# Idle tiles of queries, keys, values and probabilities take raw weight blocks in layer 0, and the loads at the change of layers are spaced two steps apart

## The chip, the core and the metric

The kernel runs on one core of a Trainium2 chip. Its engines are TensorE (PE, matmuls; PEld is its weight load), VectorE (DVE), ScalarE (ACT), GpSimd (POOL, unused here but for four constants) and the SyncE queue (SP), which issues most DMAs. The metric is the device time of one execution in microseconds (us), by the median of several runs. All times below come from a profiled execution of the kernel before or from the times of its runs.

## The reference

A trunk of two layers over 256 positions of width 2048, in float32. Layer 0 mixes by trailing-window means, layer 1 by causal attention within one block of 256 positions (there is only one block, so every selected block is masked away). Both layers have a memory branch, a SiLU gate for each branch, one output projection, a residual and a layer norm:

```python
def reference(x, mem, w_in, w_out, w_mem_kv, ln_g, ln_b, pool_w, pool_scale, w_kv_shared):
    h = x
    split_at = [BRANCH_WIDTH, 2 * BRANCH_WIDTH, 2 * BRANCH_WIDTH + MEM_WIDTH]   # 1536, 3072, 3584
    for i in range(DEPTH):                                                      # 2
        if i == N_A_LAYERS:                                                     # 1
            k_blocks, v_blocks, k_mean = moba_shared_kv(h, w_kv_shared)
        u = h @ w_in[i]                                                         # 2048 x 4096
        branch_in, gate_b, mem_q, gate_m = jnp.split(u, split_at, axis=-1)
        if i < N_A_LAYERS:
            branch = multiscale_pool(branch_in, pool_w[i], pool_scale[i])
        else:
            branch = moba_attention(branch_in, k_blocks, v_blocks, k_mean)
        mem_o = memory_attention(mem_q, mem, w_mem_kv[i])
        mixed = jnp.concatenate([branch * jax.nn.silu(gate_b), mem_o * jax.nn.silu(gate_m)], axis=-1)
        y = mixed @ w_out[i]                                                    # 2048 x 2048
        h = layer_norm(DEEPNORM_ALPHA * h + y, ln_g[i], ln_b[i])
    return h
```

Nearly all of the work is the projections: 256 rows times some 36 million weights, each weight read once from HBM.

## The kernel before

**Precision by halves.** Each float32 operand is split into a high and a low part of the type float32r (`split`, L100): ACT copies the source into the high part (L102), DVE subtracts that from the source for the low part (L103). A product is then three matmuls: high x high, high x low, low x high.

**Items and steps.** The weights are cut into blocks of 128 x 1024 float32 (512 KB). Each block is an *item* of the list `items`; the program handles them in order, one *step* for an item (`run`, L200). Step i does this, in program order: prepare item i + 3 (`prep_piece`: ACT and DVE split it into `wh`, `wl`, of which there are four pairs); issue on SP the raw loads that the plan has for step i; let TensorE consume item i (twelve matmuls of 128 x 128 by 512 columns, `proj`, L235); then run the events due at that step. `later(n, fn)` puts a function n steps ahead. Engines follow this order each for itself, held back only by data and by buffers.

**Where raw blocks land.** A raw block goes into one of four ring buffers (`raw`) or into a tile that happens to be idle, called a *slot*: the halves of the activations x, mem and z (`xh0` to `zl3`, named by `Act`, L58) serve as slots while they hold nothing. `spare` (L179) makes the plan: item after item it takes the earliest free slot (if its closing step allows) or the ring, and sets the step t of the load. A slot is free again when the item in it has been prepared, three steps before it is consumed. A load is at most `AHEAD` = 16 steps ahead of its item, and consecutive loads are at least 0.75 steps apart. *Lead* means below how many steps ahead of its own step an item is loaded. With the ring alone the lead is 7.

**The turns.** Projections come out with positions on the partitions; queries, keys, gates and layer 1's input are needed turned. `turned` (L280) and `h_turn` (L729) do it in four moves: DVE transposes 32 x 32 blocks into a tile `tr` (two of these, L264); four DMAs store it to a DRAM scratch `via` (L273); one step later one DMA brings it back in another order (L276) into `dd`, `gate` or `p`; five steps after that ACT and DVE split it (for `h_turn` ACT first applies the norm's gain and offset, L741). All of these DMAs stand on the SP queue among the raw loads.

**The change of layers.** Item 127 is the last of layer 0's output projection (mark `out0`). Items 128 to 135 are then the memory keys and 136 to 143 the memory values of layer 1 (`mem_k`, `mem_v`, marks `mk1` here not yet set, `mv1`), which need only `mem`; item 144 is the first that needs layer 1's input. Meanwhile `between` (L751) normalises and turns the four quarters of h at steps 129, 132, 135 and 138 (`normed`, `h_turn`), and at step 135 the memory keys are turned too: five turns within ten steps. The z tiles, idle from step 128 on, become slots there.

**Tiles that the change touches.** `heads_tile` (L322) makes `kk` (keys) and `qq` (queries) with high and low part in one tile of 8 KB a partition; `val_tile` (L558) makes `vv`; `ph` and `pl` hold attention weights turned and split, `p` the attention weights before that. In layer 0 `qq` also holds two of the three gates of the pooling branch (`pair`, L705). Near the end `load_gb_rows` (L799) uses `qq`, `kk` and `vv` for a few rows of the last norm's gain and offset.

Of the kernel before, what the change touches and what calls it, by code (L numbers as in the profile page):

```python
# [41 lines left out]
def trunk(ctx: ExitStack, tc: tile.TileContext, a: dict, out: bass.AP):  # L42
# [15 lines left out]
    class Act:  # L58
# [49 lines left out]
    def weave_mm(*args):  # L108
        woven.append(args)
# [29 lines left out]
    def later(n, fn):  # L139
        events[now[0] + n].append(fn)  # L140
# [35 lines left out]
    FIRST = ((0, 0, 256), (1, 0, 256), (1, 256, 512), (2, 0, 512), (0, 256, 512),  # L176
             (1, 512, 1024), (2, 512, 1024), (0, 512, 1024))

    def spare(slots):  # L179

        n = len(items)
        ring = [i - LP for i in range(RAW_BUFS)]
        ready = [o for _, o, _ in slots]
        plan = defaultdict(list)
        t = -1
        for i in range(RAW_BUFS + len(FREE), n):
            fit = [(r, k) for k, (r, (_, _, c)) in enumerate(zip(ready, slots)) if i - LP <= c]
# [12 lines left out]
    def run(slots):  # L200
        n = len(items)
        plan = spare(slots)

        def load(its):
            for it in its:
                load_piece(it, 0, it["cols"])
        for i, c0, c1 in FIRST:
            load_piece(items[i], c0, c1)
        load(items[LEAD:RAW_BUFS + len(FREE)])
        for i, c0, c1 in FIRST:  # L210
            prep_piece(items[i], c0, c1)
        load(plan[-1])
        for i in range(n):
            now[0] = i
            if i + LP < n:
                prep_piece(items[i + LP], 0, items[i + LP]["cols"])
            load(plan[i])
            it = items[i]
            if i == LEAD - 1:
                items[1]["consume"](*items[1]["w"], (0,), halves=2)  # L220
                items[2]["consume"](*items[2]["w"], (0,))
                items[1]["consume"](*items[1]["w"], (1,))
                items[2]["consume"](*items[2]["w"], (1,))
            elif i >= LEAD and it["consume"] is not None:
                it["consume"](*it["w"])
            while i in events:
# [70 lines left out]
    def in_order(tile):  # L297

        return tile.rearrange("p a (t i c) -> p (a t) i c", t=2, i=4)

    def to_heads(dst):
        def put(d):
            q = dst()
            split(in_order(q[:, 0]), in_order(q[:, 1]), d)
        return turned(put)

    def to_gate(dst):
# [8 lines left out]

    def to_values(dst):
        def done(t, acc):
            split(dst()[:, t, 0], dst()[:, t, 1], acc)
# [39 lines left out]
    class MemPair(Rows):  # L359
# [3 lines left out]
        def a(self):  # L363
            q, k = self.st["q"], self.st["k"]
            s = self.s = ps.tile([P, 2, 2, T], F32, name="s2")
            for j in range(2):
                h = self.h0 + j
                for t in range(2):
                    qh = q[:, 0, h, t * P:(t + 1) * P]
                    ql = q[:, 1, h, t * P:(t + 1) * P]  # L370
                    weave_mm(s[:, j, t], qh, k[:, 0, h], True, False)
                    weave_mm(s[:, j, t], qh, k[:, 1, h], False, False)
                    weave_mm(s[:, j, t], ql, k[:, 0, h], False, True)

        def scored(self):
            flush()
# [20 lines left out]
        def c(self):  # L397
            v = self.st["v"]
            o = self.o = ps.tile([P, 2, T], F32, name="o")
            for j in range(2):  # L400
                h = self.h0 + j
                for m in range(2):
                    vh = v[:, m, 0, h * HD:(h + 1) * HD]
                    vl = v[:, m, 1, h * HD:(h + 1) * HD]
                    e = 2 * j + m
                    weave_mm(o[:, j], vh, self.ph[:, e], m == 0, False)
                    weave_mm(o[:, j], vh, self.pl[:, e], False, False)
                    weave_mm(o[:, j], vl, self.ph[:, e], False, m == 1)

    class MobaPair(Rows):  # L410
# [5 lines left out]
        def a(self):  # L416
            q, k = self.st["q"], self.st["k"]
            s = self.s = ps.tile([P, 2, 512], F32, name="s2")
            for j in range(2):
                h = self.h0 + j  # L420
                for t, (c0, w) in enumerate(((0, P), (P, T))):
                    qh = q[:, 0, h, t * P:(t + 1) * P]
                    ql = q[:, 1, h, t * P:(t + 1) * P]
                    d = s[:, j, c0:c0 + w]
                    weave_mm(d, qh, k[:, 0, h, :w], True, False)
                    weave_mm(d, qh, k[:, 1, h, :w], False, False)
                    weave_mm(d, ql, k[:, 0, h, :w], False, True)

        def scored(self):
            flush()  # L430
# [24 lines left out]
        def c(self):  # L455
            v = self.st["v"]
            o = self.o = ps.tile([P, 2, T], F32, name="o")
            for j in range(2):
                h = self.h0 + j

                for m, (d, s) in enumerate(((o[:, j], slice(0, T)), (o[:, j, P:], slice(T, 384)))):
                    vh = v[:, m, 0, h * HD:(h + 1) * HD]
                    vl = v[:, m, 1, h * HD:(h + 1) * HD]
# [80 lines left out]
    def fresh(key, make):  # L544

        tiles = []

        def g():
            if not tiles:
                tiles.append(make())  # L550
                st[key] = tiles[0]
            return tiles[0]
        return g
# [148 lines left out]
    for c in range(3):  # L702
        proj(xT, w_in(0, c), to_pool(c))
        mark(f"pool{c}")
    pair = fresh("pair", lambda: sb.tile([P, 2, 4, T], F32, name="qq"))  # L705
    gts = [fresh("g", gate_tile), lambda: pair()[:, 0], lambda: pair()[:, 1]]
# [56 lines left out]
    after(between)  # L763
    mark("out0")
    mem_k(1)
    mem_v(1)
    after(memT.t.clear)
    mark("mv1")
# [28 lines left out]
    gbt = {}  # L797

    def load_gb_rows():  # L799
        raw = heads_tile("qq").rearrange("p h a b -> p (h a b)")[:5]  # L800
        gbt["rows"] = heads_tile("kk").rearrange("p h a b -> p (h a b)")[:5]
        gbt["hi"] = val_tile().rearrange("p a b c -> p (a b c)")[:5]
        gbt["sel"] = gbsel
        nc.scalar.dma_start(gbt["sel"], a["sel"])
        for nm, p0, p1 in (("ln_g", 0, 3), ("ln_b", 3, 5)):
            nc.scalar.dma_start(f(raw)[p0:p1], a[nm][1][None, :].to_broadcast([p1 - p0, D]))
        for n in range(4):
            later(5 + n, lambda n=n: split_rows(f(raw)[:, n * 512:(n + 1) * 512], n))

    def split_rows(raw, n):  # L810
        hi, rows = (gbt[k][:, n * 512:(n + 1) * 512] for k in ("hi", "rows"))
        nc.scalar.activation(hi, raw, AF.Copy)
        nc.vector.tensor_scalar_mul(f(hi), f(hi), gbt["sel"][:, 0:1])
        nc.vector.scalar_tensor_tensor(rows, raw, gbt["sel"][:, 1:2], f(hi),
                                       op0=ALU.mult, op1=ALU.add)

    main = collect(out_cols, 1, 0, 1) + collect(out_cols, 1, 2)
# [16 lines left out]
    for part in range(2):  # L834
        for q in range(4):
# [75 lines left out]
    ts = {}  # L911
    for n in (1, 2, 3):
        ts[n] = ps.tile([P, 512], F32, name="acc", bufs=4)
        mm(ts[n], cct, gbt["rows"][:, n * 512:(n + 1) * 512], True, True)
# [62 lines left out]
```

## Time and profile before

| | us |
|---|---|
| median of 3 runs | 811.78 |
| lowest and highest run | 810.54, 812.57 |
| the profiled execution itself | 812.46 |
| its span in the profile | 810.7 |
| busy in it: DVE, ACT | 546.7, 389.9 |
| HBM read | 173.37 MB |

The span is what the profile covers from the first to the last instruction; the execution's own time holds 1.8 us more. "Busy" is the time in which an engine had an instruction running. A line of the profile names source line, engine and operation, `out<-in` by the names of tiles, sizes, and for a timeline in brackets how long the engine was idle before and what released it. In the part on DMA queues, "landing" is the time from the issue of a DMA to its arrival.

### The profile page before, as it was taken

To read this page: it belongs to the slowest core of one execution; us is meant where nothing else is said; L and a number is where in the kernel's file an instruction comes from. 1 tells how busy PE (TensorE), PEld (TensorE's weight loads), DVE (VectorE), ACT (ScalarE), POOL (GpSimd) and SP (SyncE) were. 2 spreads that over 40 slices of the span, in tenths; PEclk is the share of its full clock that TensorE was granted. 3 is DMA by queue.
4 is the path that set the end of the run, shared out by engine and by line. 5 is a ranking of instruction groups with operands and counts; after the bars stand their busy time and mean duration, and the time that the engine had idled before them with its cause. 6 is when DMAs were issued, how large, how long until landed. Compare 5 with 4: busy or idle time off the path is not lost.

```text
span 810.7 us, 10039 instructions
## 1 busy us (share of the span) xinstructions
PE 793.0 (98%) x3671; PEld 661.0 (82%) x3671; DVE 546.7 (67%) x710; ACT 389.9 (48%) x502; POOL 0.2 (0%) x4
## 2 busy tenths in 40 slices
PE   7999999999999999998999999999999999999996
PEld 6888888888888888886788888888888888888785
DVE  5666677768765665656668777666577565765936
ACT  6545545544454433675545545454455354554510
POOL 0000000000000000000000000000000000000000
PEclk9999999999999999999999999999999999999998
DMA  8999666666687765689998876858656875746632
GB/s 319 332 379 306 204 214 210 224 216 202 197 282 267 258 197 194 205 257 297 376 341 267 280 245 223 282 170 286 223 174 202 242 243 203 247 150 212 227 102 104
DMA packets 96181, 193.69 MB, mean 239 GB/s; under 512 B 8672, under 2 KB 31488, under 8 KB 95872
## 3 DMA queue, kind: packets, MB, share of 16 engines
q1 hardware_dynamic: 94800, 190.61, 70.4%
q10 hardware_dynamic: 1332, 2.46, 0.9%
q8 instruction: 28, 0.46, 0.2%
q14 instruction: 21, 0.16, 0.1%
HBM read 173.37 MB, written 19.66 MB: 238 GB/s over the span
## 4 chain that ended last, share of the span: by engine, by line
PE 89%; DMA 6%; DVE 2%; SPq 1%; ACT 1%; issue 1%; ACTq 0%; DVEq 0%
PE acc L98 84%; DMA via<-tr 3%; PE o L98 2%; PE s L98 2%; DVE wl L103 1%; DMA raw<-in_w_mk 1%; DMA dd<-via 1%; DMA raw<-in_w_out 1%; ACT wh L102 1%; PE pt L98 1%; DMA p<-via 0%; SPq L273 0%; SPq L150 0%; DVE xl L103 0%; SPq L148 0%
## 5 line engine op out<-in xcount | busy, mean ns | idle before, releaser
L98 PE MATMUL acc<-wl,xh 128*128 128x512 f32 x704 | 276.4, 393 | 1.0 <-DVE wl L103 1.0
L98 PE MATMUL acc<-wh,xh 128*128 128x512 f32 x704 | 276.1, 392 | 1.2 <-ACT wh L102 1.2
L98 PE MATMUL acc<-wh,xl 128*128 128x512 f32 x704 | 276.4, 393 | 0.0
L103 DVE TENSOR_TENSOR wl<-raw,wh 128x1024 fp32r<-128x1024 f32 (+4 forms) x155 | 180.6, 1176 | 96.4 <-ACT wh L102 94.5
L102 ACT ACTIVATE wh<-raw 128x1024 fp32r<-128x1024 f32 (+4 forms) x155 | 157.1, 1022 | 150.4 <-PE acc L98 116.4
L98 PEld LDWEIGHTS acc<-wh,xh 128*128 128x128 f32 x704 | 132.6, 188 | 29.6 <-ACT wh L102 1.7
L98 PEld LDWEIGHTS acc<-wl,xh 128*128 128x128 f32 x704 | 132.5, 188 | 29.3 <-DVE wl L103 2.1
L98 PEld LDWEIGHTS acc<-wh,xl 128*128 128x128 f32 x704 | 132.6, 188 | 27.9
L98 PE MATMUL acc<-wl,zh 128*128 128x512 f32 x224 | 87.5, 391 | 0.3 <-DVE wl L103 0.3
L98 PE MATMUL acc<-wh,zl 128*128 128x512 f32 x224 | 87.5, 390 | 0.0
L98 PE MATMUL acc<-wh,zh 128*128 128x512 f32 x224 | 87.4, 390 | 0.0
L103 DVE TENSOR_TENSOR wl<-zh,wh 128x1024 fp32r<-128x1024 f32 x38 | 46.4, 1224 | 32.4 <-ACT wh L102 30.8
L103 DVE TENSOR_TENSOR wl<-zl,wh 128x1024 fp32r<-128x1024 f32 x39 | 47.1, 1219 | 20.4 <-ACT wh L102 20.4
L102 ACT ACTIVATE wh<-zh 128x1024 fp32r<-128x1024 f32 x38 | 40.0, 1057 | 38.3 <-PE acc L98 36.2
L98 PE MATMUL acc<-wh,mh 128*128 128x512 f32 (+1 forms) x130 | 51.8, 398 | 5.0 <-ACT wh L102 5.0
L102 ACT ACTIVATE wh<-zl 128x1024 fp32r<-128x1024 f32 x39 | 40.7, 1055 | 32.2 <-PE acc L98 32.1
L98 PE MATMUL acc<-wl,mh 128*128 128x512 f32 (+1 forms) x130 | 52.1, 401 | 2.6 <-DVE wl L103 2.6
L98 PE MATMUL acc<-wh,ml 128*128 128x512 f32 (+1 forms) x130 | 51.3, 395 | 0.0
L98 PEld LDWEIGHTS acc<-wl,zh 128*128 128x128 f32 x224 | 42.1, 188 | 9.4 <-DVE wl L103 0.7
L98 PEld LDWEIGHTS acc<-wh,zl 128*128 128x128 f32 x224 | 42.0, 188 | 8.8
L98 PEld LDWEIGHTS acc<-wh,zh 128*128 128x128 f32 x224 | 42.1, 188 | 8.7
L102 ACT ACTIVATE zh<-zf 128x256 fp32r<-128x256 f32 x32 | 13.0, 415 | 53.2 <-DVE zf L329 48.7
(152 smaller groups left out, 761.2 us busy)
## 6 DMA issues: line engine op xcount, KB each, us to landing
raw<-in_w_in SPq DMA_DIRECT2D x59, 512.0 KB, 5.6
raw<-in_w_out SPq DMA_DIRECT2D x58, 512.0 KB, 4.4
via<-tr SPq DMA_DIRECT2D x116, 128.0 KB, 4.0
zh<-in_w_in SPq DMA_DIRECT2D x26, 512.0 KB, 8.2
zl<-in_w_in SPq DMA_DIRECT2D x25, 512.0 KB, 6.9
dd<-via SPq DMA_DIRECT2D x21, 512.0 KB, 3.8
raw<-in_w_mk SPq DMA_DIRECT2D x10, 512.0 KB, 4.9
mh<-in_w_sk SPq DMA_DIRECT2D x10, 512.0 KB, 8.3
```

Source lines behind the costliest of these rows:

```text
L98: nc.tensor.matmul(o, l, r, start=start, stop=stop)
L102: nc.scalar.activation(hi, src, AF.Copy)
L103: nc.vector.tensor_sub(lo, src, f(hi))
```

## The change

It does four things.

1. Nine tiles become slots for raw blocks: `qqh`, `qql`, `kkh`, `kkl`, `vv0`, `vv1`, `ph`, `pl`, `p`, each from the step at which layer 0 is done with it (the keys 16 steps after mark `q0`, values and attention weights 28 steps after it, the queries after the last pooling mix, a new mark `mix`) until layer 1 needs it (new mark `mk1`).
2. `spare` takes a new argument `calm` = step 127: a load placed from there to 14 steps on is at least 2 steps after the one before it, elsewhere 0.75 as before.
3. Keys, queries and values become two tiles each of 4 KB a partition (high and low part; for the values one for each half of the positions). What reads and writes them is rewritten with the same shapes.
4. `load_gb_rows` loads its gain and offset rows in two halves each: four DMAs on the ACT queue in place of two.

```diff
-    def spare(slots):
+    def spare(slots, calm):
...
-            t = max(r, i - AHEAD, t + (0.75 if t >= 0 else 0))
+            t = max(r, i - AHEAD, t + (0 if t < 0 else 2 if 0 <= t - calm < 14 else 0.75))
...
     def heads_tile(name):
-        return sb.tile([P, 2, 4, T], F32R, name=name)
-
+        return [sb.tile([P, 4, T], F32R, name=name + part) for part in "hl"]
...
     def val_tile():
-        return sb.tile([P, 2, 2, 512], F32R, name="vv")
+        return [sb.tile([P, 2, 512], F32R, name=f"vv{t}") for t in range(2)]
...
-    items.extend(main[:5] + mixes[2] + main[6:11] + mixes[3] + main[5:6] + main[11:])
+    items.extend(main[:5] + mixes[2] + main[6:11] + mixes[3])
+    mark("mix")
+    items.extend(main[5:6] + main[11:])
...
     mem_k(1)
+    mark("mk1")
     mem_v(1)
...
     def load_gb_rows():
-        raw = heads_tile("qq").rearrange("p h a b -> p (h a b)")[:5]
...
+        flat = lambda tiles: [x.rearrange("p a b -> p (a b)")[:5] for x in tiles]
+        raw, gbt["rows"], gbt["hi"] = flat(heads_tile("qq")), flat(heads_tile("kk")), flat(val_tile())
+        nc.scalar.dma_start(gbsel, a["sel"])
         for nm, p0, p1 in (("ln_g", 0, 3), ("ln_b", 3, 5)):
-            nc.scalar.dma_start(f(raw)[p0:p1], a[nm][1][None, :].to_broadcast([p1 - p0, D]))
+            for i in range(2):
+                nc.scalar.dma_start(f(raw[i])[p0:p1], a[nm][1, i * 1024:(i + 1) * 1024][None, :].to_broadcast([p1 - p0, 1024]))
...
-    run(slots)
+    for nm in ("qqh", "qql", "kkh", "kkl", "vv0", "vv1", "ph", "pl", "p"):
+        start, stop = {"q": (at("mix") + 1, at("q1") + 5), "k": (at("q0") + 16, at("mk1") + 5),
+                       "v": (at("q0") + 28, at("mv1")), "p": (at("q0") + 28, at("q1") + 15)}[nm[0]]
+        slots.append((lambda nm=nm: sb.tile([P, BLK], F32, name=nm), start, at("out0") + 5 if nm == "p" else stop))
+    run(slots, at("out0"))
```

The plan of loads follows from this by the rule of `spare`, and the order of the DMAs on SP shows it. Before, on SP, from the last pooling block to the end of layer 1's memory keys; `raw` is the ring, `zh` the first idle z tiles:

```order
L150 DMA raw<-in_pool_b 128x384
L150 DMA raw<-in_w_out 128x1024 x22
L148 DMA raw<-in_w_mk 128x2x512 x7
L148 DMA zh_2795<-in_w_mk 128x2x512
L150 DMA zh_2797<-in_w_mv 128x1024
L150 DMA zh_2819<-in_w_mv 128x1024
```

and in the changed program, a piece of the same place:

```order
L150 DMA qqh<-in_w_out 128x1024
L150 DMA qql<-in_w_out 128x1024
L150 DMA raw<-in_w_out 128x1024 x4
L150 DMA kkh<-in_w_out 128x1024
L150 DMA kkl<-in_w_out 128x1024
L148 DMA vv_2509<-in_w_mk 128x2x512
L148 DMA vv_2529<-in_w_mk 128x2x512
L148 DMA ph<-in_w_mk 128x2x512
L148 DMA pl<-in_w_mk 128x2x512
L148 DMA p<-in_w_mk 128x2x512
L148 DMA qqh<-in_w_mk 128x2x512
L148 DMA qql<-in_w_mk 128x2x512
```

The ring's four buffers are now joined by nine tiles in turn. The second place is the change of layers on SP, from the turn of h's second quarter on. Before (`via<-tr` are the stores of a turn, four for each; `gate`, `p` and `dd` take what comes back; `in_w_mv` and `in_w_in` are weights):

```order
L273 DMA via<-tr 32x4x256 x4
L150 DMA zl_2914<-in_w_mv 128x1024
L276 DMA p<-via 128x1024
L150 DMA raw<-in_w_mv 128x1024
L148 DMA raw<-in_w_in 128x2x512 x2
L273 DMA via<-tr 32x4x256 x8
L148 DMA raw<-in_w_in 128x2x512
L276 DMA dd<-via 128x1024
L276 DMA gate<-via 128x1024
L148 DMA zh_3019<-in_w_in 128x2x512
L148 DMA zh_3021<-in_w_in 128x2x512
L148 DMA zh_3045<-in_w_in 128x2x512
```

and in the changed program from the same turn to the end of the last one:

```order
L273 DMA via<-tr 32x4x256 x4
L148 DMA zh_2926<-in_w_in 128x2x512
L276 DMA p<-via 128x1024
L148 DMA zh_2967<-in_w_in 128x2x512
L273 DMA via<-tr 32x4x256 x8
L276 DMA dd<-via 128x1024
L276 DMA gate<-via 128x1024
L148 DMA zl_3025<-in_w_in 128x2x512
L273 DMA via<-tr 32x4x256 x4
L148 DMA zl_3076<-in_w_in 128x2x512
L276 DMA p<-via 128x1024
L148 DMA zl_3119<-in_w_in 128x2x512
```

The turns stand in the same order; between the first of these stores and the return into `gate` there were five weight blocks and are now two, and the three blocks behind that return have become one. The third place is ACT near the end, where the rows of the last norm are loaded (`small` takes a selection, `qq` the gain and offset rows, `xh` is a kept weight block). Before:

```order
L102 ACTIVATE wh<-raw 128x1024 x2
L804 DMA small<-in_sel 5x2
L806 DMA qq<-in_ln_g 3x2048
L806 DMA qq<-in_ln_b 2x2048
L102 ACTIVATE xh_408<-raw 128x1024
```

and now:

```order
L102 ACTIVATE wh<-raw 128x1024 x2
L800 DMA small<-in_sel 5x2
L803 DMA qqh<-in_ln_g 3x1024
L803 DMA qql<-in_ln_g 3x1024
L803 DMA qqh<-in_ln_b 2x1024
L803 DMA qql<-in_ln_b 2x1024
L102 ACTIVATE xh_408<-raw 128x1024
```

Two DMA issues more stand ahead of the next cast.

More of the change, by code (lines that the diff above doesn't have):

```diff
@@ L198, in spare, with run @@
         return plan
-    def run(slots):
+    def run(slots, calm):
         n = len(items)
-        plan = spare(slots)
+        plan = spare(slots, calm)
         def load(its):
@@ L303, in put @@
             q = dst()
-            split(in_order(q[:, 0]), in_order(q[:, 1]), d)
+            split(in_order(q[0]), in_order(q[1]), d)
         return turned(put)
@@ L318, in done @@
         def done(t, acc):
-            split(dst()[:, t, 0], dst()[:, t, 1], acc)
+            split(dst()[t][:, 0], dst()[t][:, 1], acc)
         return done
     def heads_tile(name):
-        return sb.tile([P, 2, 4, T], F32R, name=name)
+        return [sb.tile([P, 4, T], F32R, name=name + part) for part in "hl"]
     def gated(o, g, kt):
@@ L368, in a @@
                 for t in range(2):
[L369 to L373, printed above, removed]
+                    qh, ql = (x[:, h, t * P:(t + 1) * P] for x in q)
+                    weave_mm(s[:, j, t], qh, k[0][:, h], True, False)
+                    weave_mm(s[:, j, t], qh, k[1][:, h], False, False)
+                    weave_mm(s[:, j, t], ql, k[0][:, h], False, True)
         def scored(self):
@@ L402, in c @@
                 for m in range(2):
-                    vh = v[:, m, 0, h * HD:(h + 1) * HD]
-                    vl = v[:, m, 1, h * HD:(h + 1) * HD]
+                    vh, vl = (v[m][:, i, h * HD:(h + 1) * HD] for i in range(2))
                     e = 2 * j + m
@@ L421, in a @@
                 for t, (c0, w) in enumerate(((0, P), (P, T))):
-                    qh = q[:, 0, h, t * P:(t + 1) * P]
-                    ql = q[:, 1, h, t * P:(t + 1) * P]
+                    qh, ql = (x[:, h, t * P:(t + 1) * P] for x in q)
                     d = s[:, j, c0:c0 + w]
-                    weave_mm(d, qh, k[:, 0, h, :w], True, False)
-                    weave_mm(d, qh, k[:, 1, h, :w], False, False)
-                    weave_mm(d, ql, k[:, 0, h, :w], False, True)
+                    weave_mm(d, qh, k[0][:, h, :w], True, False)
+                    weave_mm(d, qh, k[1][:, h, :w], False, False)
+                    weave_mm(d, ql, k[0][:, h, :w], False, True)
         def scored(self):
@@ L461, in c @@
                 for m, (d, s) in enumerate(((o[:, j], slice(0, T)), (o[:, j, P:], slice(T, 384)))):
-                    vh = v[:, m, 0, h * HD:(h + 1) * HD]
-                    vl = v[:, m, 1, h * HD:(h + 1) * HD]
+                    vh, vl = (v[m][:, i, h * HD:(h + 1) * HD] for i in range(2))
                     weave_mm(d, vh, self.ph[:, j, s], m == 0, False)
@@ L704, in trunk @@
         mark(f"pool{c}")
-    pair = fresh("pair", lambda: sb.tile([P, 2, 4, T], F32, name="qq"))
-    gts = [fresh("g", gate_tile), lambda: pair()[:, 0], lambda: pair()[:, 1]]
+    pair = fresh("pair", lambda: [sb.tile([P, 4, T], F32, name="qq" + part) for part in "hl"])
+    gts = [fresh("g", gate_tile), lambda: pair()[0], lambda: pair()[1]]
     mixes = [collect(pool_mix, g, gts) for g in range(4)]
@@ L799, in load_gb_rows, with rows_of @@
     def load_gb_rows():
-        raw = heads_tile("qq").rearrange("p h a b -> p (h a b)")[:5]
[L801 to L804, printed above, removed]
+        flat = lambda tiles: [x.rearrange("p a b -> p (a b)")[:5] for x in tiles]
+        raw, gbt["rows"], gbt["hi"] = flat(heads_tile("qq")), flat(heads_tile("kk")), flat(val_tile())
+        nc.scalar.dma_start(gbsel, a["sel"])
         for nm, p0, p1 in (("ln_g", 0, 3), ("ln_b", 3, 5)):
-            nc.scalar.dma_start(f(raw)[p0:p1], a[nm][1][None, :].to_broadcast([p1 - p0, D]))
+            for i in range(2):
+                nc.scalar.dma_start(f(raw[i])[p0:p1], a[nm][1, i * 1024:(i + 1) * 1024][None, :].to_broadcast([p1 - p0, 1024]))
         for n in range(4):
-            later(5 + n, lambda n=n: split_rows(f(raw)[:, n * 512:(n + 1) * 512], n))
+            later(5 + n, lambda n=n: split_rows(f(raw[n // 2])[:, n % 2 * 512:n % 2 * 512 + 512], n))
+    def rows_of(key, n):
+        return gbt[key][n // 2][:, n % 2 * 512:n % 2 * 512 + 512]
     def split_rows(raw, n):
-        hi, rows = (gbt[k][:, n * 512:(n + 1) * 512] for k in ("hi", "rows"))
+        hi, rows = (rows_of(k, n) for k in ("hi", "rows"))
         nc.scalar.activation(hi, raw, AF.Copy)
-        nc.vector.tensor_scalar_mul(f(hi), f(hi), gbt["sel"][:, 0:1])
-        nc.vector.scalar_tensor_tensor(rows, raw, gbt["sel"][:, 1:2], f(hi),
+        nc.vector.tensor_scalar_mul(f(hi), f(hi), gbsel[:, 0:1])
+        nc.vector.scalar_tensor_tensor(rows, raw, gbsel[:, 1:2], f(hi),
                                        op0=ALU.mult, op1=ALU.add)
@@ L913, in trunk @@
         ts[n] = ps.tile([P, 512], F32, name="acc", bufs=4)
-        mm(ts[n], cct, gbt["rows"][:, n * 512:(n + 1) * 512], True, True)
+        mm(ts[n], cct, rows_of("rows", n), True, True)
     nc.vector.scalar_tensor_tensor(r0, r0, rs, b0, op0=ALU.mult, op1=ALU.add)
```

## Prediction

> **What bounds the kernel now.** I read the page first, then what TensorE waited for, then the one stretch in which it waited, engine by engine. On the page, its head and its first engine:
>
> ```profile
> span 810.7 us, 10039 instructions
> PE 793.0 (98%) x3671; PEld 661.0 (82%) x3671; DVE 546.7 (67%) x710; ACT 389.9 (48%) x502; POOL 0.2 (0%) x4
> ```
>
> TensorE is busy for 793.0 of 810.7 us, so nothing that another engine does faster can gain more than the 17.7 us that are left, unless matmuls themselves ran slowly. The list of what PE waited for, over the whole span and then from 340 to 400 us (total, times, longest):
>
> ```profile
> PE acc L98 <- ACT wh L102: 6.2, 2, 5.0
> PE acc L98 <- DVE wl L103: 3.9, 5, 2.4
> ...
> PE acc L98 <- DVE wl L103: 3.4, 3, 2.4
> PE acc L98 <- ACT wh L102: 1.2, 1, 1.2
> ```
>
> Of 6.2 + 3.9 us, 5.0 lie at the very start (the longest wait, for the first weights). Of the other 5.1 us, 4.6 (3.4 + 1.2) lie in one stretch, the change of layers. TensorE's timeline there (start, duration, idle before and its releaser):
>
> ```profile
> 370.13 0.39 PE L98 MATMUL acc<-wh,mh 128*128 128x512 f32 x1
> 372.89 0.50 PE L98 MATMUL acc<-wl,mh 128*128 128x512 f32 x1 [2.38 <-DVE wl L103]
> 380.46 0.50 PE L98 MATMUL acc<-wl,xh 128*128 128x512 f32 x1 [0.21 <-DVE wl L103]
> 383.09 0.39 PE L98 MATMUL acc<-wh,xh 128*128 128x512 f32 x1
> 385.81 0.39 PE L98 MATMUL acc<-wh,xh 128*128 128x512 f32 x1
> 389.93 0.49 PE L98 MATMUL acc<-wh,xh 128*128 128x512 f32 x1 [1.24 <-ACT wh L102]
> 391.19 0.75 PE L98 MATMUL acc<-wl,xh 128*128 128x512 f32 x1 [0.76 <-DVE wl L103]
> ```
>
> Two stalls: 2.38 + 0.21 us (items 142 and 144) and 1.24 + 0.76 us (item 147), together 4.59. From 383.09 to 385.81 stand the twelve matmuls of one item, 2.72 us, or 0.227 us each. Behind each stall they come more slowly for a while, as the granted clock shows (third figure from the end):
>
> ```profile
> 372.00:376.00 4.00, 3.10 (x10) 2.51 (x11) 2.01 (x3) 1.06 (x1) 0.00 (x0) 0.78 1.01 350
> 376.00:380.00 4.00, 4.00 (x16) 3.08 (x14) 2.01 (x2) 3.88 (x6) 0.00 (x0) 0.80 0.97 253
> 388.00:392.00 4.00, 2.00 (x7) 1.13 (x6) 2.09 (x2) 4.00 (x6) 0.00 (x0) 0.91 0.95 342
> 392.00:396.00 4.00, 4.00 (x13) 3.14 (x13) 3.68 (x4) 2.07 (x3) 0.00 (x0) 0.66 1.05 408
> ```
>
> The clock lost 0.22, 0.20, 0.09 and 0.34 of these slices of 4 us: 0.88 + 0.80 + 0.36 + 1.36 = 3.40 us, behind each stall about half. So the change of layers costs 4.59 + 3.40 = **8.0 us**, and of PE's waits for weights all but 0.5 us lie in it or at the start. That is all a change to loads can gain.
>
> **Why it stalls.** What DVE, then ACT, then the SP queue did around both stalls:
>
> ```profile
> 355.14 1.31 DVE L264 STREAM_TRANSPOSE tr<-acc 128x512 f32<-128x512 f32 x2
> 364.42 1.23 DVE L103 TENSOR_TENSOR wl<-zl,wh 128x1024 fp32r<-128x1024 f32 x1 [1.54 <-ACT wh L102]
> 369.29 1.30 DVE L264 STREAM_TRANSPOSE tr<-res 128x512 f32<-128x512 f32 x2 [3.65 <-DMA via<-tr]
> 371.62 1.22 DVE L103 TENSOR_TENSOR wl<-zl,wh 128x1024 fp32r<-128x1024 f32 x1
> ...
> 361.36 2.08 ACT L741 ACTIVATE p<-p,gcol 128x256 f32<-128x256 f32 x4 [2.16 <-DMA p<-via]
> 386.86 2.08 ACT L741 ACTIVATE p<-p,gcol 128x256 f32<-128x256 f32 x4 [3.91 <-DMA p<-via]
> 388.84 1.04 ACT L102 ACTIVATE wh<-zh 128x1024 fp32r<-128x1024 f32 x1
> ...
> 347.97 2.65 SPq L273 DMA_DIRECT2D via<-tr  x4
> 358.09 0.34 SPq L276 DMA_DIRECT2D p<-via  x1
> 383.37 0.34 SPq L276 DMA_DIRECT2D p<-via  x1
> ```
>
> Both engines work in program order. For the first stall, DVE stands 3.65 us before the transposes of h's last quarter (369.29), since their buffer `tr` still holds what an earlier store to `via` is reading; the low half of item 142's weights comes behind, at 371.62, and PE starts at 372.89. For the second, ACT waits 3.91 us for that quarter to come back (`p<-via`, issued only at 383.37), then makes four pieces of it, and item 147's high half starts at 388.84. Either way a small transfer was late, not a block of weights. Landing times from 332 to 396 us, and then those from 60 to 330 (last column, median us):
>
> ```profile
> raw<-in_w_in SPq DMA_DIRECT2D x7, 512.0 KB, 8.3
> via<-tr SPq DMA_DIRECT2D x20, 128.0 KB, 7.9
> ...
> via<-tr SPq DMA_DIRECT2D x40, 128.0 KB, 3.0
> ```
>
> A store takes 7.9 us here and 3.0 elsewhere. The queue is full here:
>
> ```profile
> 340.00:396.00 56.00, 51.40 (x209) 41.07 (x208) 34.72 (x36) 35.53 (x48) 0.00 (x0) 0.94 0.86 281
> 395.00:430.00 35.00, 35.00 (x161) 29.19 (x160) 24.50 (x27) 15.06 (x15) 0.00 (x0) 1.00 0.99 344
> ```
>
> The cause is the planner: in most of layer 0 it has only the ring, so the eight steps from 128 on start 7 items ahead; then the z tiles come free and it goes to 16 ahead just here, with four loads in three steps (0.75 apart), among the five turns.
>
> **The change, part by part.** (1) *More landing places in layer 0.* Nine tiles join the slots. By the rule of `spare`, item 128 is now loaded 16 steps ahead instead of 7, and the lead never falls under 9 before item 266. That adds no instruction: as many raw blocks, of the same 512 KB, with the same casts. Catching up costs 45 loads in steps 47 to 89 instead of 38; 7 x 512 KB over 43 x 2.72 = 117 us is 31 GB/s, beside the 281 of the row, in a layer without a stall: I take 0, bounds 0 and one stall as above (2.59 + 1.70 = 4.3). (2) *Half the loads at the change of layers.* Steps 128 to 141 issue 8 loads instead of 19. From the first store to the last `p<-via` SP issues 5 instead of 13: 8 x 0.52 = 4.2 MB less, 15 us of transfer at the 281 GB/s of the row.
>
> Do the stalls go? First stall: the stores that these transposes wait for are ready for SP at 356.5, when the row at 355.14 has written `tr`; but SP is held until 358.09 by the return of an earlier quarter, whose own store, out by 350.6, was late too. With stores of 3.0 us that return goes out at 353.6, the four stores by 356.5 + 2.65 = 359.1, and they land at 362. DVE comes to the transposes at 365.65, when the row at 364.42 ends, so its 3.65 us vanish; the stall that they caused is 2.59, so 1.06 are to spare, and 1.54 more, which DVE waits for ACT at 364.42, itself held by another `p<-via` at 361.36. Second stall: the last store starts 3.65 + 1.54 = 5.2 us earlier and lands 7.9 - 3.0 = 4.9 us faster; 2.0 are needed. What is late next? Nothing of ACT or DVE: they are busy for 35.5 and 34.7 of the 56 us in the row from 340. The blocks: item 150 is loaded 9 steps ahead, 24.5 us; landing 8.3 and the two casts 2.3 leave 13.9 for SP to be late. So **both stalls go, and with them the clock**: -4.59 - 3.40 = -8.0. Bounds: 0 (stores as slow as now) and -8.0. The value is -8.0, since the nearest row for a store among about one load a step is 3.0, and up to about 6 both deadlines still hold.
>
> [...]
>
> (3) *Catching up later.* Steps 142 to 175 issue 40 loads, before 38, and the DMA engines were at 0.99 from 395 to 430 already, with no stall. I take 0; bounds 0 and 4.3. (4) *Tiles in two halves, views alike.* Instructions on PE and DVE are of the same shapes; 0. (5) *Two more DMA issues on ACT near the end.*
>
> ```profile
> 742.84 0.28 ACTq L806 DMA_DIRECT2D qq<-in_ln_b  x1
> 744.01 1.04 ACT L102 ACTIVATE xh<-raw 128x1024 fp32r<-128x1024 f32 x1
> ...
> 762.43 0.50 PE L98 MATMUL acc<-wl,zh 128*128 128x512 f32 x1 [0.31 <-DVE wl L103]
> ```
>
> The cast behind them starts at 744.01, when the one before it ends; the issues end at 743.12. Two more of 0.28 end at 743.68, still 0.33 ahead: 0. Without that cover up to 0.56, in a place where PE lacks only 0.31. (6) *An added wait.* The first load into `kkh`, at step 47, waits on SP for the score matmuls that read the keys. Behind it stand a load needed 12 steps later, and the turn of item 47's own result, which PE makes later anyway: 0.
>
> Sum: span 810.7 - 8.0 = 802.7. Outside the span lie 812.46 - 810.7 = 1.76, so the profiled execution would be 804.5; it lay 0.68 over the median of the runs, 811.78. By the median: **803.8**.
>
> **Rivals.**
> - *One stall stays* (one chain is longer than I see): 811.8 - 4.3 = 807.5 or 811.8 - 3.7 = 808.1. For it: the second chain has two transfers and ACT's work in a row. Against: the spare time above. 0.08.
> - *The clock does not come back with the gaps*: -4.6 alone, 807.2. Against it, each drop stands right behind a stall, and from 395 on the row shows 1.00. [...] 0.03.
> - *The tail gets worse*: lead 9 instead of 11 for items 255 to 259, ACT's two issues; 803.8 + 0.56 + 1.7 for a half clock = 806.1. 0.03.
> - *It does not do what it says*: stores wait for their own kind (eight in a row) and not for the loads, so they stay at 7.9 and both stalls stay: 811.8. For it: in the changed order those eight still stand together. Against: as many stores elsewhere need 3.0. 0.08.
> - *Slower: the thinned stretch starves PE.* Place: items 150 and 151, which stand behind the last `p<-via` on SP. If stores stay slow, both stalls stay, and if SP is held by one more of 7.9, item 150 comes late. It decides at 13.9 us of lateness of SP against PE; before, `p<-via` went out at 383.37, 13.2 after item 142 should have run (370.1). One more store: 13.2 + 7.9 - 13.9 - 4.6 (PE's own stalls) = 2.6, with a half clock 1.7: 811.8 + 4.3 = 816.1. 0.06.
>
> **How the numbers follow.** Forecast 803.8 with 0.72. About 0.3% (2.4 us) is what a measurement of this kernel can tell from no change. Faster than 809.4: 0.72 + 0.08 + 0.03 + 0.03 = 0.86; within: 0.08; slower: 0.06. The range goes from 802.8 (the runs before lie up to 1.2 us under their median; about 1 taken) to 808.2, which takes in one remaining stall, the clock and the tail, and leaves 0.14 and a little out.
>
> **What the next profile would show.** Right: no PE wait between 20 and 755 us, the granted clock 1.00 in every slice there, stores around 340 to 380 us landing in 3 to 4.5 us, PE busy time about 790 (793.0 - 3.4). Wrong: stores still near 7.9; a half clock without a gap; PE waiting on ACT for blocks near item 150, or anywhere from 390 to 460, where loads are made up for; a longer gap near 754.

## The result and the profile after

The changed kernel takes 804.76 us (median of 4 runs, 804.36 to 806.05); the kernel before took 811.47 in the runs beside it. The ratio is 0.992, with an interval of 0.9902 to 0.9937. In a second comparison it was 803.78 against 810.6, 0.9916 (0.9901 to 0.9931). The profiled execution took 804.36, with a span of 802.4 where the one before had 810.7.

The head of the page of the changed kernel, and the list of what its TensorE waited for (total us, times, longest):

```profile
span 802.4 us, 10035 instructions
PE 789.7 (98%) x3671; PEld 659.8 (82%) x3671; DVE 546.2 (68%) x710; ACT 390.1 (49%) x502; POOL 0.2 (0%) x4
```

```profile
PE acc L98 <- ACT wh L102: 4.6, 2, 4.4
PE pt L912 <- DVE cc L909: 2.8, 1, 2.8
PE acc L98 <- ACT cct L914: 0.4, 1, 0.4
```

PE's busy time fell by 3.3 us with the same 3671 matmuls, about the 3.40 that the half clock took before. The line of waits for `wl`, 3.9 us before, is gone, and what is left lies in the first 7 us and in the last 10. The stretch that held the loss, by engine over 56 us, and two of the slices where the clock had been down (third figure from the end: granted clock; then DMA share and GB/s):

```profile
340.00:396.00 56.00, 56.00 (x249) 46.39 (x248) 40.76 (x42) 39.53 (x52) 0.00 (x0) 1.00 0.81 265
372.00:376.00 4.00, 4.00 (x19) 3.30 (x19) 2.33 (x3) 4.00 (x6) 0.00 (x0) 1.00 0.50 164
388.00:392.00 4.00, 4.00 (x19) 3.31 (x18) 1.74 (x2) 1.80 (x2) 0.00 (x0) 1.00 1.03 362
```

Before, the row from 340 read 51.40 busy, 209 matmuls, clock 0.94. The 4.59 us of stalls, 3.40 of half clock and the gap of 0.31 that stood at 762.43 make 8.30, and 810.7 - 802.4 is 8.3. That this fits so well is luck. The first matmul of layer 1's memory keys, and the first of layer 1's output projection (it reads `zh`), before and then in the changed kernel:

```profile
332.05 0.39 PE L98 MATMUL acc<-wh,mh 128*128 128x512 f32 x1
709.81 0.39 PE L98 MATMUL acc<-wh,zh 128*128 128x512 f32 x1
```

```profile
333.08 0.39 PE L98 MATMUL acc<-wh,mh 128*128 128x512 f32 x1
701.89 0.39 PE L98 MATMUL acc<-wh,zh 128*128 128x512 f32 x1
```

From the one to the other it took 377.76 us and takes 368.81: 8.95 less, not 7.99. A gap cost more than its idle time where it can be read: at 13.18 us in the kernel before, where matmuls start every 0.227 us, a gap of 0.21 stands between starts at 12.58, 13.18 and 13.51, so 0.93 us for two steps, 0.48 more than usual. In return, the profiled execution of the changed kernel was already 1.03 us late at its memory keys, because at its start the matmuls came 0.43 us apart until 12.06 us, before only until about 9.

The two chains of the prediction in the changed kernel: DVE's transposes, then ACT's work on returned quarters of h, then the SP queue.

```profile
357.40 1.26 DVE L264 STREAM_TRANSPOSE tr<-res 128x512 f32<-128x512 f32 x2
364.32 1.30 DVE L264 STREAM_TRANSPOSE tr<-res 128x512 f32<-128x512 f32 x2
```

```profile
370.61 2.08 ACT L738 ACTIVATE gate<-gate,gcol 128x256 f32<-128x256 f32 x4 [2.68 <-DMA gate<-via]
377.34 2.07 ACT L738 ACTIVATE p<-p,gcol 128x256 f32<-128x256 f32 x4
```

```profile
354.22 0.34 SPq L276 DMA_DIRECT2D p<-via  x1
357.50 4.50 SPq L273 DMA_DIRECT2D via<-tr  x8
362.17 0.34 SPq L276 DMA_DIRECT2D dd<-via  x1
...
373.38 0.34 SPq L276 DMA_DIRECT2D p<-via  x1
```

The transposes at 364.32, 369.29 before, carry no bracket: they wait for nothing. The last return is issued at 373.38 and not at 383.37, and the ACT work behind it, which waited 3.91, waits no more. Landing times from 332 to 396 us, and for the stores from 60 to 330 (last column):

```profile
via<-tr SPq DMA_DIRECT2D x20, 128.0 KB, 3.2
...
via<-tr SPq DMA_DIRECT2D x40, 128.0 KB, 4.9
```

A store at the change of layers lands in 3.2 us by the median; it was 7.9. The trace gives the landing of only some of the twenty (6 now, 14 before), and in the changed kernel they spread from 2.3 to 6.2. The last four stores alone, those of h's last quarter, before and now:

```profile
via<-tr SPq DMA_DIRECT2D x4, 128.0 KB, 8.9
```

```profile
via<-tr SPq DMA_DIRECT2D x4, 128.0 KB, 6.2
```

In layer 0, where 45 loads now make up the lead, it takes 4.9; it was 3.0. The stores have got slower there and nothing waits for them.

### The profile page after: what moved, and what is told of

It reads as the page before. It is cut to its first block, busy times and chain, and to the rows that moved or that the text cites. A ratio compares the mean times of both kernels' runs of the same rounds, so it can differ in the third digit from the quotient of the medians.

```text
span 802.4 us, 10035 instructions
## 1 busy us (share of the span) xinstructions
PE 789.7 (98%) x3671; PEld 659.8 (82%) x3671; DVE 546.2 (68%) x710; ACT 390.1 (49%) x502; POOL 0.2 (0%) x4
## 4 chain that ended last, share of the span: by engine, by line
PE 95%; DVE 2%; DMA 1%; issue 0%; ACT 0%; SPq 0%; DVEq 0%; ACTq 0%
PE acc L98 91%; PE o L98 2%; PE s L98 2%; DMA raw<-in_w_out 1%; DVE wl L103 1%; DMA raw<-in_w_mk 1%; PE pt L98 1%; ACT wh L102 0%; DVE res L924 0%; DVE xl L103 0%; DVE res L477 0%; DVE zf L328 0%; DVE res L905 0%; DVE stats L478 0%; DVEq L977 0%
## 5 line engine op out<-in xcount | busy, mean ns | idle before, releaser
L103 DVE TENSOR_TENSOR wl<-raw,wh 128x1024 fp32r<-128x1024 f32 (+4 forms) x109 | 126.6, 1168 | 67.0 <-ACT wh L102 66.7
L102 ACT ACTIVATE wh<-raw 128x1024 fp32r<-128x1024 f32 (+4 forms) x109 | 110.1, 1016 | 110.1 <-PE acc L98 92.1
L103 DVE TENSOR_TENSOR wl<-zh,wh 128x1024 fp32r<-128x1024 f32 x35 | 42.7, 1222 | 24.7 <-ACT wh L102 23.2
L103 DVE TENSOR_TENSOR wl<-zl,wh 128x1024 fp32r<-128x1024 f32 x34 | 41.2, 1220 | 21.6 <-ACT wh L102 20.1
L102 ACT ACTIVATE wh<-zh 128x1024 fp32r<-128x1024 f32 x35 | 36.9, 1056 | 33.7 <-PE acc L98 33.7
L102 ACT ACTIVATE wh<-zl 128x1024 fp32r<-128x1024 f32 x34 | 35.5, 1056 | 25.5 <-PE acc L98 22.4
```

What stands on the lines that cost most here:

```text
L102: nc.scalar.activation(hi, src, AF.Copy)
L103: nc.vector.tensor_sub(lo, src, f(hi))
```

## The experiments

One table for the runs without added gaps. The first three experiments below ran beside a median of 811.72 for the kernel before, the others beside 810.6, so ratios can be compared and medians only within each group. "Idle" is PE's idle time between 300 and 700 us, "clock" the time lost to the granted clock between 240 and 440 (its shortfall from 1.00 times the slice), both in the profiled execution, added up from rounded slices; "store" is the median landing time of the turns' stores from 332 to 396 us, "last four" that of h's last quarter; "keys to z" is the time between the two matmuls shown above.

| kernel | store | last four | idle | clock | keys to z | span | median | ratio to before (interval) |
|---|---|---|---|---|---|---|---|---|
| before | 7.9 | 8.9 | 4.59 | 3.40 | 377.76 | 810.7 | 811.78 | |
| changed, again | 2.9 | 6.2 | 0 | 0 | 368.81 | 802.6 | 803.78 | 0.9916 (0.9901 to 0.9931) |
| halves only | 8.2 | 8.6 | 5.65 | 1.72 | 377.61 | 810.4 | 811.91 | 1.0003 (0.9989 to 1.0018) |
| slots only | 6.5 | 7.8 | 2.38 | 0 | 372.06 | 805.2 | 807.43 | 0.9949 (0.9933 to 0.9964) |
| thinned a little, no slots | 6.3 | 9.1 | 2.36 | 0 | 372.10 | 805.2 | 806.62 | 0.9947 (0.9932 to 0.9962) |
| a load every 4th step | 3.8 | 4.1 | 0.83 | 0 | 370.59 | 803.6 | 806.34 | 0.9949 (0.9932 to 0.9965) |
| last quarter in its own buffer | 7.2 (without the last four) | 9.9 | 5.44 | 1.72 | 377.48 | 811.1 | 811.86 | 1.0012 (1.0002 to 1.0021) |
| turns on GpSimd's queue | 6.0 | 6.6 | 5.18 | 5.16 | 379.77 | 813.1 | 814.91 | 1.0054 (1.0039 to 1.0069) |

Idle and clock together explain most of "keys to z": over the 368.81 of the changed kernel they leave 0.6 to 1.5 us, or 0.16 to 0.48 for each gap. The spans hold the start as well, where the profiled executions differ by up to 1.1 us.

**Slots only.** The changed kernel with the old spacing of 0.75 steps everywhere: 14 loads in steps 128 to 141 (before 19, changed 8), lead 16.

```diff
-            t = max(r, i - AHEAD, t + (0 if t < 0 else 2 if 0 <= t - calm < 14 else 0.75))
+            t = max(r, i - AHEAD, t + (0 if t < 0 else 0.75))
```

> The changed kernel with the old spacing of 0.75 throughout: the nine slots alone. Lead 16 at the change of layers, 14 loads in steps 128 to 141 (before 19, changed 8). Theory, the number of loads among the turns decides: stores land between the 3.2 us of the changed kernel and the 7.9 of before, by proportion 3.2 + 4.7 x 6/11 = 5.8 us; at most one stall is left: 805 to 808.5. Rival, the lead alone decides (the blocks are there early, so late turns do no harm): no stall, 804.8. Rival, the spacing alone decides: 811.5.

Measured: 807.43. One stall of two is left, at item 144. What ACT did ahead of it, and PE:

```profile
372.79 1.06 ACT L102 ACTIVATE kkh<-dd 128x1024 fp32r<-128x1024 f32 x1 [6.94 <-DMA dd<-via]
374.46 2.08 ACT L738 ACTIVATE gate<-gate,gcol 128x256 f32<-128x256 f32 x4 [0.61 <-DMA gate<-via]
```

```profile
377.53 0.50 PE L98 MATMUL acc<-wh,xh 128*128 128x512 f32 x1 [1.62 <-ACT wh L102]
378.79 0.50 PE L98 MATMUL acc<-wl,xh 128*128 128x512 f32 x1 [0.76 <-DVE wl L103]
```

With 14 loads among the turns and stores of 6.5 us, small transfers still make a stall, but now two that the prediction did not speak of: the return of the memory keys (`dd<-via`) and, last to come, that of h's third quarter (`gate<-via`, 0.61 us after the keys were cast). Without the wait for the keys ACT would still have stood until 374.46. The slots alone bring some 60% of the gain: 811.72 in the runs of before beside it, less 807.43, is 4.3 of 6.8 us.

**Thinned a little, without slots.** The kernel before, with loads at least 1 step apart instead of 0.75 in the 14 steps from mark `out0`: 15 loads, and the lead stays at 7.

```diff
-            t = max(r, i - AHEAD, t + (0.75 if t >= 0 else 0))
+            t = max(r, i - AHEAD, t + (0 if t < 0 else 1 if 0 <= t - calm < 14 else 0.75))
```

> The kernel before, with a spacing of 1 step in place of 0.75 in the 14 steps from the change of layers on and nothing else: the lead stays 7, 15 loads in steps 128 to 141, almost as many as with the slots alone (14). Theory, the number of loads decides: as the slots alone, 805 to 808.5, stores at about 6 us. Rival, the lead decides: as before, 811.5, both stalls.

Measured: 806.62, as good as the slots alone, with one number changed and no new landing place. So a high lead is not what helps; it is fewer loads among the turns. What remains has another cause. ACT in this kernel:

```profile
369.46 1.06 ACT L102 ACTIVATE wh<-raw 128x1024 fp32r<-128x1024 f32 x1 [4.15 <-DMA raw<-in_w_mv]
...
376.03 1.06 ACT L102 ACTIVATE wh<-raw 128x1024 fp32r<-128x1024 f32 x1 [1.51 <-DMA raw<-in_w_in]
```

ACT now waits for blocks of weights, the second time right ahead of PE's stall at 377.14 (1.29 us, then 0.77). With a lead of 7, the thinned loads came late themselves. That is a use of the slots: they build the lead beforehand, in layer 0, which the thinned stretch then spends, and in the changed kernel no such wait is left. Half the loads without the slots was not run. The second stall is gone here although the last four stores took 9.1 us: they start at 368.40 and not at 372.89, so when a store starts counts too, not only how long it takes.

**Halves only.** The changed kernel with neither the nine slots nor the spacing.

```diff
-    for nm in ("qqh", "qql", "kkh", "kkl", "vv0", "vv1", "ph", "pl", "p"):
...
-            t = max(r, i - AHEAD, t + (0 if t < 0 else 2 if 0 <= t - calm < 14 else 0.75))
+            t = max(r, i - AHEAD, t + (0 if t < 0 else 0.75))
```

> The changed kernel without the nine slots and with the old spacing: tiles in halves and the four gain and offset loads on the ACT queue are all that is left of the change. Theory: as before, 811.5, both stalls, since no load moves. Rival, the finer tiles free ACT and DVE from waits on each other: 804.8 or part of the way. Rival for the end: the two more DMA issues on ACT cost up to 0.56 us near 750: 812.

Measured: 811.91, ratio 1.0003. Two tiles in place of one and the two more DMA issues cost nothing that can be measured. Its profile has more idle time than before (5.65 us, not 4.59) and less of the half clock (1.72, not 3.40); the section on the hardware comes back to that.

**The last quarter in its own buffer.** The kernel before; `h_turn` transposes h's last quarter into the idle tile `zl3` instead of `tr`, and that tile becomes a slot only 16 steps after `out0`. This takes away what DVE waited 3.65 us for ahead of the first stall.

```diff
-        tr = sb.tile([P, 4, 256], F32, name="tr", bufs=2)
+        tr = sb.tile([P, 4, 256], F32, name="zl3") if n == 3 else sb.tile([P, 4, 256], F32, name="tr", bufs=2)
...
-            slots.append((z, at("out0") + 1, at("q1") + 16 if q == 3 else at(f"moba{q}") + 17))
+            slots.append((z, at("out0") + (16 if (part, q) == (1, 3) else 1), at("q1") + 16 if q == 3 else at(f"moba{q}") + 17))
```

> The kernel before, with the transposes of h's last quarter going into an idle z tile in place of the two tr buffers, so that they wait for no earlier store; as many loads as before (19). Theory of the two stalls: the first one (2.6 us of idle, with the clock up to 4.3) goes, since DVE no longer waits there; the second stays, since the last store and its return stand where they stood on SP: 807.5 to 809. Rival, both stalls have one cause on SP and the buffer is no matter: 811.5. Rival, both go: 804.

Measured: 811.86, no faster; the expectation missed. DVE, then ACT:

```profile
365.56 1.30 DVE L264 STREAM_TRANSPOSE zl<-res 128x512 f32<-128x512 f32 x2
```

```profile
373.88 1.06 ACT L102 ACTIVATE kk<-dd 128x1024 fp32r<-128x1024 f32 x1 [6.65 <-DMA dd<-via]
...
387.55 2.08 ACT L741 ACTIVATE p<-p,gcol 128x256 f32<-128x256 f32 x4 [4.92 <-DMA p<-via]
```

DVE's wait is gone as planned, and the stall at 372.89 with it; but ACT then waits 6.65 us for the memory keys and another 0.86, until 375.80, for h's third quarter (`gate<-via`), and PE stalls at 378.87 for 2.44 and 0.76 us. In the kernel before, these waits of ACT are there too (7.64 us, at 374.87, then 0.19), hidden behind the first stall. Three small transfers are late, and freeing one lets the next decide.

**The turns on another queue.** The kernel before, with the stores and returns of steps 127 to 144 issued from GpSimd instead of SP. If SP's order makes them late, they should land as fast as elsewhere; if the DMA engines are full, not.

```diff
+    def queue():
+        return nc.gpsimd if 127 <= now[0] < 145 else nc.sync
...
-                nc.sync.dma_start(st["via"][:, :, i].rearrange("j r x -> r j x"), tr[32 * i:32 * i + 32, :, :n])
+                queue().dma_start(st["via"][:, :, i].rearrange("j r x -> r j x"), tr[32 * i:32 * i + 32, :, :n])
...
-            nc.sync.dma_start(land(), st["via"].rearrange("j r i x -> (j r) i x"))
+            queue().dma_start(land(), st["via"].rearrange("j r i x -> (j r) i x"))
```

> The kernel before, with the turns' DMAs of steps 127 to 144 (five turns, stores and returns) issued on the GpSimd queue, which is idle, in place of SP; the 19 loads stay where they were. Theory A, a store is late because it stands behind loads in SP's own queue: stores at 3 to 4 us, both stalls gone, 804 to 806. Theory B, the DMA engines themselves are full, whatever the queue: stores stay at 7 to 8 us, both stalls stay, 811.5. Not known: what issuing from GpSimd costs by itself.

Measured: 814.91, slower. Landing times from 332 to 396 us:

```profile
via<-tr POOLq DMA_DIRECT2D x20, 128.0 KB, 6.0
gate<-via POOLq DMA_DIRECT2D x2, 512.0 KB, 6.5
...
dd<-via POOLq DMA_DIRECT2D x1, 512.0 KB, 8.0
```

On a queue of their own the stores still take 6.0 us, between the forecasts of the two theories (3 to 4, 7 to 8). SP is no longer held up by them, so it sends its loads earlier: from 340 to 396 us the DMA engines move 309 GB/s, before 281. ACT waits 6.16 us for `gate<-via`, and a stall appears at 360.60 that was not there. This speaks against SP's order as the only cause and for what the DMA engines have to do. It is not clean, since SP's loads moved too and a GpSimd DMA may have a price of its own: only the sum was measured.

**A load every fourth step.** The changed kernel with 4 in place of 2: three loads in the stretch, and a lead of 4 to 6 for items 147 to 155. It looks for the rival on the other side, blocks that come late.

```diff
-            t = max(r, i - AHEAD, t + (0 if t < 0 else 2 if 0 <= t - calm < 14 else 0.75))
+            t = max(r, i - AHEAD, t + (0 if t < 0 else 4 if 0 <= t - calm < 14 else 0.75))
```

> The changed kernel with a load every fourth step in place of every second at the change of layers: 3 loads in steps 128 to 141, and a lead that falls to 4 at item 147 and 5 to 6 up to item 155 (in the changed kernel 9). Theory, the thinned stretch can starve PE: item 147 is loaded in step 143 and has 4 x 2.72 = 10.9 us until PE is due there, less 2.3 for the casts leaves 8.6, and loads in this stretch landed in 6 to 12; PE waits for blocks, 1 to 5 us with the clock, 806 to 810. Rival, the fewer loads the better, since the turns are what is late: 804.8 or less.

Measured: 806.34, between before and changed. That lies in the theory's range, but not by its mechanism: PE does not wait for a block there even with a lead of 4. What it lost in the profile lies 80 us later:

```profile
474.07 0.38 PE L98 MATMUL o<-pl,vv 128*128 128x256 f32 x1 [0.52 <-DVE pl L103]
487.54 0.33 PE L98 MATMUL s<-kkh,qql 128*128 128x128 f32 x1 [0.31 <-DVE qql L103]
```

These stand in layer 1's attention, behind ACT's wait of 5.80 us at 471.70 for `p<-via`: the deferred loads may be what meets other turns there. So two steps is not too much, and four is. The profiled execution (805.35, span 1.0 longer than the changed kernel's) shows only part of the 2.6 us between the medians; the other runs, 804.55 to 808.43, were not profiled, so what the rest is stays open.

**Gaps made on purpose.** The changed kernel, which has no gap between 7 us and the end, with blocks of 32 x 32 transposes on DVE that nothing reads; PE waits for the weights behind them. The first kernel has 13 to 19 transposes a block and was run once:

```diff
+    def block(n):
+        x, y = (sb.tile([P, 512], F32, name=nm) for nm in ("ln_g", "ln_b"))
+        nc.vector.memset(x, 0.0)
+        for _ in range(n):
+            blocks(y, x)
+    for s, n in ((107, 13), (112, 15), (117, 17), (122, 19)):
+        later(s, lambda n=n: block(n))
```

> The changed kernel with extra work on VectorE alone at four quiet steps of layer 0 (107, 112, 117, 122): one memset and 13, 15, 17, 19 transposes of 128x512 of 0.61 us each, that is 7.9, 9.2, 10.4 and 11.6 us. PE can go on for about 7.6 us without VectorE, so it should be idle for about 0.3, 1.6, 2.8 and 4.0 us. Reading of this case's trace: idle time of about 2 us or more within 3.4 us brings a half clock, so the last two gaps bring 1.7 us each, and the second perhaps; in all 804.8 + 8.7 + 3.4 = 816.9, up to 818.6. [...] Rival, the clock falls for another reason than the gaps: 813.5.

Measured: 835.46. The transposes took 0.71 us each on average (64 of them 45.6) and not 0.61 (the next expectation takes 0.74), so the gaps were 2.90, 7.15, 5.61 and 7.44 us. The one of 2.90 was followed by 1.72 us of lost clock, each of the others by about 3.4. The second kernel, also run once, has four blocks of 12, at steps 100, 106, 115 and 122; the question is again which gaps bring a half clock:

> The changed kernel with four blocks of 12 transposes of 32 x 32 tiles added on DVE (into a tile that nothing reads), at steps 100, 106, 115 and 122, where TensorE otherwise never waits; the output stays the reference's. By the 0.74 us of a transpose and the cover of some 7.3 us that the sizes with 13 to 19 transposes showed, each block of 8.9 us should leave TensorE a gap of about 1.6 to 2.2 us. [...] Theory C, the length of the gap alone decides at a bound under 2 us: all four bring it, 819.

Measured: 819.89. The sizes missed again, which happened to help: the same block left two long gaps and two short ones. The time is near Theory C's 819 only by that; its sum is not for these gaps.

```profile
274.30 0.58 PE L98 MATMUL pt<-zh,wl 128*128 128x256 f32 x1 [4.71 <-DVE wl L103]
293.69 0.50 PE L98 MATMUL acc<-wl,zh 128*128 128x512 f32 x1 [3.73 <-DVE wl L103]
322.02 0.50 PE L98 MATMUL acc<-wl,zh 128*128 128x512 f32 x1 [1.91 <-DVE wl L103]
343.26 0.50 PE L98 MATMUL acc<-wl,zh 128*128 128x512 f32 x1 [1.91 <-DVE wl L103]
```

The first two each cost 1.72 us of clock, the two of 1.91 none, so a bound under 2 us (Theory C) does not hold. 12.26 of gaps and 3.44 of clock on 802.5 make 818.2; the span is 818.0.

## Why the prediction was right, point by point

- **The bound and the stretch**: right. All of the profiled gain but a few tenths lies in the change of layers. The terms (4.59 idle, 3.40 clock) are there; what a stall costs beyond its idle time, 0.96 us in all, the sum put at nothing.
- **The cause** (stores land late because too many loads stand among the turns, so fewer loads bring both stalls away): that fewer loads among the turns bring the stalls away is right, and shown by the row of runs: 19 loads, stores of 7.9 us and two stalls; 14 and 15 loads, 6.5 and 6.3 and one (the second of these for a weight block); 8 loads, 3 and none; 3 loads, 3.8 and none there. Why a load makes a store late is not shown. The GpSimd run speaks for full DMA engines and does not settle it. The mean share of the engines from 340 to 396 us hardly tells the kernels apart (0.86 before, 0.81 now), and at 407.35 in the kernel before four stores landed in 4.9 us with the engines at 1.05 from 404 to 408.
- **The chain of the second stall**: right in sum, partly by luck. The prediction let the last four stores start 5.2 us earlier and land in 3.0 us, together 10.1 us gained; they start 7.2 us earlier (365.65) and land in 6.2, and the last return goes out at 373.38, 10.0 us earlier. Only 2.0 were needed. "Up to about 6 both deadlines still hold" is borne out by these 6.2; that all stores would land in 3 to 4.5 is not.
- **The chain of the first stall**: too narrow. The prediction followed DVE's wait for `tr` alone and asked "what is late next?" only of engines and blocks. The run with its own buffer shows the answer, two returns: ACT waits 6.65 us for the memory keys and then 0.86 for h's third quarter. The change works because it mends all of these transfers at once: ACT no longer waits for the keys and the last quarter, and 2.68 us for the third quarter without a stall of PE.
- **The size**: the prediction took 8.0 us from the median, and the medians differ by 6.7 and 6.8. The forecast of 803.8 is 1.0 under the first median (804.76) and meets the second (803.78) only because the kernel before was faster there too. The term that is mis-sized most is the clock. The profiled execution of before had a mean granted clock of 0.992, as low as any of the 39 timed executions beside the experiments: two of them show 0.992, and their mean is 0.9954. The eight of the changed kernel have 0.996. So an ordinary execution of before lost some 0.0006 x 811 = 0.5 us more to the clock than the changed kernel, not 3.40. An estimate from these terms, 4.59 + 0.5 + 0.96 for what gaps cost besides + 0.31 for the gap at 762.43, is 6.36 us. It is rough: the 5 to 7 us at half clock at the very end of both kernels alone move a mean by 0.001, which is 0.8 us, and halves only, which moves no load, shows 5.65 of idle and 1.72 of clock. For the profile 804.5 was predicted and 804.36 came, but there 8.95 us gained and a start 1.03 us later cancel.
- **Slots cost nothing in layer 0**: right; stores there went from 3.0 to 4.9 us without a stall.
- **Catching up later, halves, ACT's two issues, the added wait**: 0 each, right as far as PE's waits show it (only the halves with ACT's issues were run alone). No wait stands in the list between the first 7 us and the last 10; the halves alone gave 1.0003; the gap of 0.31 at 762.43, which the prediction feared to see grow, is gone.
- **The rivals**: the clock that does not come back is refuted by 1.00 in the whole stretch, and stores that wait for their own kind by the load counts above, with twenty stores each time. One stall that stays is what half of the change gives. Blocks that come late near items 150 and 151 were not seen with a lead of 4 to 6; with thinning and no slots they were, at item 144 (the ACT wait of 1.51 us).

## What to carry to other kernels

When a small transfer on the way of a tuned pipeline lands late, look at how many bulk loads the planner puts beside it, and move those to a stretch with less traffic (in the kernel before, a DMA share of 0.69 from 60 to 330 us against 0.86 from 340 to 396); moving one number of the planner was worth some 5 of 6.8 us here. Before freeing one buffer for one named waiter, list every wait of that stretch on every engine, also those that are hidden behind it, since in the run with its own buffer the next late one took over (ACT's 6.65 us). A median over many transfers can hide the one that counts (3.2 us for the twenty stores, 6.2 for the last four). And a loss by the clock that one profile shows need not be that of the other runs (here a mean clock of 0.992 in the profile, 0.9954 over 39 executions): set the profile's mean clock beside those of the timed runs before taking it from a median.

## What the runs showed of the hardware

A stretch at half clock is called a drop here. In these profiles drops did not follow from the length of a gap alone. In the kernel before, gaps of 2.38 and of 1.24 + 0.76 us were each followed by one; in halves only, 2.73 was not and 0.81 + 0.76 was; in slots only, 1.62 + 0.76 was not; above, 1.91 twice was not. So what the first run with gaps was expected to show, that some 2 us of idle or more brings a half clock, does not hold. Quarters of a microsecond in the first run with gaps, at the start of each drop:

```profile
289.50:289.75 0.25, 0.25 (x1) 0.21 (x2) 0.25 (x1) 0.00 (x0) 0.00 (x0) 0.78 0.00 0
310.00:310.25 0.25, 0.00 (x0) 0.00 (x0) 0.21 (x2) 0.00 (x0) 0.00 (x0) 0.74 0.00 0
330.50:330.75 0.25, 0.00 (x0) 0.00 (x0) 0.25 (x1) 0.00 (x0) 0.00 (x0) 0.70 0.00 0
354.25:354.50 0.25, 0.00 (x0) 0.00 (x0) 0.25 (x1) 0.00 (x0) 0.00 (x0) 0.98 0.00 0
```

A slice that shows 0.78 was at full clock until 0.11 us before its end, when read as a mean of 1.00 and 0.50: the drops begin at 289.64, 310.12, 330.60 and 354.49. They lie 20.48, 20.48 and 23.89 us apart, which is 6, 6 and 7 times 3.413. The two drops of the kernel before (374.21 and 391.27) lie 17.06 us apart, 5 times that, the two of the last run (273.78 and 294.26) 20.48, 6 times. The drop at the end of the kernel before, at 804.28 (the slice from 804.25 to 804.50 shows 0.57), comes 413.01 us after the one at 391.27, 121 times that. What sets these distances is not shown.

Cut into pieces of 3.413 us, counted from the drops, each profile shows what PE did ahead of a drop. The kernel before, then halves only, then the last run (columns: piece, length, PE busy with matmuls in brackets, and so on; clock third from the end):

```profile
370.80:374.21 3.41, 1.31 (x6) 1.09 (x7) 3.17 (x3) 0.00 (x0) 0.00 (x0) 1.00 0.89 271
374.21:377.62 3.41, 3.41 (x10) 2.67 (x9) 1.22 (x1) 2.56 (x5) 0.00 (x0) 0.50 1.01 324
```

```profile
388.58:391.99 3.41, 1.84 (x7) 1.02 (x6) 2.25 (x2) 3.41 (x5) 0.00 (x0) 1.00 1.00 368
391.99:395.40 3.41, 3.41 (x9) 2.66 (x9) 3.41 (x4) 1.60 (x3) 0.00 (x0) 0.50 1.05 408
```

```profile
318.15:321.57 3.42, 1.95 (x9) 1.30 (x7) 3.31 (x5) 1.16 (x2) 0.00 (x0) 1.00 0.01 2
321.57:324.98 3.41, 2.96 (x13) 2.47 (x14) 3.41 (x4) 0.14 (x1) 0.00 (x0) 1.00 0.47 170
```

A piece in which PE never waited has some 16 or 17 matmuls. Ahead of all twelve drops in six profiles stands a piece with 0 to 7 (the last 20 us are left out, where the matmuls are smaller); of the pieces cut, none with 8 or more was followed by a drop, and with 7 it went both ways (a few records of matmuls can be missing). The idle time of a piece does not tell them apart: 1.57 us came ahead of a drop in halves only and 1.62 in the GpSimd run, while in halves only the 1.82 that one piece got of the gap of 2.73 (the piece before got 0.91) brought none. Eight of the drops lasted one piece, 3.41 us, and cost 1.7 us, half of it; the other four, whose first piece was itself thin (4, 1, 3 and 5 matmuls), lasted two. That such gaps went both ways could be why the kernels that kept one stall vary more from run to run: 804.96 to 810.12 for the thinned one and 805.52 to 809.67 for slots only, in ten runs each, against 0.8 and 1.7 us in four runs each of the changed kernel. The slowest thinned run has the lowest mean clock of its ten, 0.993, but of the two slowest of slots only (809.67 and 809.65) one has 0.995 and one 0.992. They were not profiled, so this is not shown.
